# Batched matmul on one core: from a scheduled kernel to one critical section with hand-made waits, a TensorE loop, one load per stationary tile and the first x in one transfer

## The chip, the core and the metric

The kernel runs on one NeuronCore of a Trainium2 chip. Five engines work side by side, each with its own instruction stream: TensorE (PE; its weight loads have a row of their own, PEld), VectorE (DVE), ScalarE (ACT), GpSimd (POOL) and SyncE (SP). Here POOL and SP issue the transfers, which 16 DMA engines carry out. The metric is device time in microseconds of the whole launch; lower is better. Three runs of the kernel before took 513.78, 513.84 and 513.95 us, a median of 513.84 us.

## The reference

```python
batch, m, k, n = 32, 512, 1024, 768
x      = randn(batch, m, k)   float32
weight = randn(batch, k, n)   float32
out = np.matmul(x, weight)    # float32, (32, 512, 768)
```

The 32 matrices of weight are all different, so nothing is used twice across batches: 167.77 MB are read and 50.33 MB are written.

## The kernel before, in words

**Layout.** P is 128, MT = 4 tiles of rows, KT = 8 tiles of the contraction. A weight matrix is read as float32 and stored as bf16 by the transfer itself (1.5 MB in SBUF, 3.1 MB in memory). x is read in the same way; batches 1 and 2, 3 and 4, up to 29 and 30 are read in pairs, with batch 2p+1 in the lower and 2p+2 in the upper 64 partitions (L57, `load_pair`), and batch 31 alone (L62). Batch 0's x stays float32: three of its four row tiles come in one transfer from SP (L169), the fourth in 18 small ones of 16, 2 or 5 rows (L170 to L172).

**TensorE.** x must be turned before it can be the stationary operand. `words` (L74) transposes two bf16 at a time as if they were one float32: four transposes into one PSUM tile, eight such groups for a pair of batches. DVE copies each group into xT (L96; L93 and L94 for the last pair, L101 for batch 31, L115 for batch 0). `matmuls` (L128) then does, for each of 4 row tiles and 8 contraction tiles, two matmuls on the same stationary tile, 512 and 256 columns wide; each has its own weight load. So a batch has 64 matmuls and 64 loads. For batch 28 (`CHUNKED`, L29) the weight comes as two transfers, and the first half of the contraction is done for all row tiles before the second.

**Emptying PSUM.** Two row tiles share three PSUM banks. `evacuate` (L151) copies them to out_sb: ACT takes banks 0 and 2, DVE bank 1, each in two halves of 64 partitions (L163), whole for the batches 30 and 31 (L154 to L156).

**Order.** The order within each engine is written out by hand (`manual_schedule`, L165); the waits are put in by the framework from the pools: 4 weight buffers, 3 x buffers, 3 out buffers of a pair of batches, 6 of xT. POOL's queue holds, at an odd batch b: x of the pair that begins at b+4 (L190), the store of the pair that ended at b-2 (L192), the weight of b+3 (L194); at an even b only the weight of b+3. The weight of b+3 goes into the buffer of b-1, so it waits for the matmuls of b-1. The x of a pair takes the buffer of three pairs before, whose transposes are long done. From batch 26 on no store is issued until b = 28, when two are (L196, L197). The last stores are on SP: half of batch 30, the pair 28 and 29, the other half of 30, and two halves of 31 (L200 to L202, L232).

Of the kernel before, what the change touches and what calls it, by code (L numbers as in the profile page):

```python
# [13 lines left out]
def kernel(  # L14
# [9 lines left out]
    P = 128  # L24
    MT = M // P
# [3 lines left out]
    CHUNKED = {B - 4: (4, 4)}  # L29
    AHEAD = 3  # L30
    LATE = 4
    HELD = 3

    const = ctx.enter_context(tc.tile_pool(name="const", bufs=1))
    w_pool = ctx.enter_context(tc.tile_pool(name="w", bufs=4))
    x_pool = ctx.enter_context(tc.tile_pool(name="x", bufs=3))
    xT_pool = ctx.enter_context(tc.tile_pool(name="xT", bufs=6))
    out_pool = ctx.enter_context(tc.tile_pool(name="out", bufs=3))
    one_pool = ctx.enter_context(tc.tile_pool(name="one", bufs=1))
    tpsum = ctx.enter_context(tc.tile_pool(name="tpsum", bufs=2, space=bass.MemoryType.PSUM))  # L40
    mpsum = ctx.enter_context(tc.tile_pool(name="mpsum", bufs=2, space=bass.MemoryType.PSUM))

# [7 lines left out]
    xs, ws, outs, twos = {}, {}, {}, {}  # L52

    def banks():
        return [mpsum.tile([P, 512], F32, name=f"pm{i}") for i in range(3)]

    def load_pair(b):  # L57

        xs[b] = x_pool.tile([P, 2 * MT, K], BF16, name="x_sb")
        nc.gpsimd.dma_start(out=xs[b], in_=pair_view[b // 2])  # L60

    def load_last():  # L62
        xs[B - 1] = x_pool.tile([P, MT, K], BF16, name="x_sb")
        nc.gpsimd.dma_start(out=xs[B - 1], in_=x_view[B - 1])

    def load_w(b):
        ws[b] = w_pool.tile([P, KT, N], BF16, name="w_sb")
        at = 0
        for n in CHUNKED.get(b, (KT,)):
            nc.gpsimd.dma_start(out=ws[b][:, at:at + n, :], in_=w_view[b, :, at:at + n, :])  # L70
            at += n


    def words(b, mo):  # L74
        pt = tpsum.tile([P, JT, P], F32, name="pt")
        pairs = xs[b].bitcast(F32)
        for j in range(JT):
            nc.tensor.transpose(pt[:, j, :], pairs[:, mo, j::JT], ident)  # L78
        return pt.bitcast(BF16)

    def transpose_pair(b, mt):

        both = xT_pool.tile([P, 2, JT, 2, P // 2, 2], BF16, name="xT")
        in_rows = [both[:, r].rearrange("p j h i r -> p j (h i) r") for r in range(2)]
        if b + 1 == B - 2:

            in_rows[1] = both[:, 1].rearrange("p j h i r -> p j (h i r)").rearrange(
                "p j (m r) -> p j m r", r=2
            )
        for half in range(2):  # L90
            pt = words(b, mt + MT * half).rearrange("p j (b i r) -> p j b i r", b=2, r=2)
            if b + 1 == B - 2:
                nc.vector.tensor_copy(both[:, 0, :, half], pt[:, :, 0])  # L93
                nc.vector.tensor_copy(in_rows[1][:, :, half::2, :], pt[:, :, 1])  # L94
            else:
                nc.vector.tensor_copy(both[:, :, :, half].rearrange("p b j i r -> p j b i r"), pt)  # L96
        return in_rows

    def transpose_last(mt):
        xT = xT_pool.tile([P, JT, P, 2], BF16, name="xT")  # L100
        nc.vector.tensor_copy(  # L101
            xT.rearrange("p j m r -> p (j m r)"), words(B - 1, mt).rearrange("p j m -> p (j m)")
        )
        return xT

    def transpose_first(mt):

        xT = xT_pool.tile([P, JT, P, 2], BF16, name="xT")
        rows = x_first[:, mt] if mt < MT - 1 else x_fourth[:, 0]
        for h in range(2):  # L110
            pt = tpsum.tile([P, JT, P], F32, name="pt")
            for i in range(JT):
                nc.tensor.transpose(pt[:, i, :], rows[:, JT * h + i::KT], ident)  # L113
            for j in range(2):
                nc.vector.tensor_copy(  # L115
                    xT[:, 2 * h + j].rearrange("p (h i) r -> p r h i", h=2),
                    pt[:, 2 * j:2 * j + 2].rearrange("p r (i h) -> p r h i", h=2),
                )
        return xT


# [6 lines left out]
    def matmuls(pm, half, xT, b, kos, together):  # L128
        for ko in kos:
            for i, (bank, at, off, size) in enumerate(SPLITS[half]):  # L130
                shares = half == 1 and i == 0
                nc.tensor.matmul(  # L132
                    pm[bank][:, at:at + size],
                    xT[:, ko // 2, :, ko % 2],
                    ws[b][:, ko, off:off + size],
                    start=(ko == 0 and not (together and shares)),
                    stop=(ko == KT - 1),
                    skip_group_check=together,
                )

    def open_out(b):

        if b == B - 2:
            outs[b] = one_pool.tile([P, MT * N], F32, name="one_sb")
            return
        if b % 2 == 0 or b == B - 1:
            twos[b // 2] = out_pool.tile([P, 2 * MT * N], F32, name="out_sb")
        if b == B - 1:
            outs[b] = twos[b // 2][:, :MT * N]

    def evacuate(b, pair, pm):  # L151
        if b >= B - 2:
            o = outs[b][:, pair * N2:(pair + 1) * N2]
            nc.scalar.copy(o[:, 0:512], pm[0])  # L154
            nc.vector.tensor_copy(o[:, 512:1024], pm[1])  # L155
            nc.scalar.copy(o[:, 1024:N2], pm[2])  # L156
            return
        H = P // 2
        mine = twos[b // 2][H * (b % 2):H * (b % 2 + 1)]
        for i, copy in enumerate((nc.scalar.copy, nc.vector.tensor_copy, nc.scalar.copy)):  # L160
            for h in range(2):
                at = pair * N2 + h * MT * N + 512 * i
                copy(mine[:, at:at + 512], pm[i][H * h:H * (h + 1)])  # L163

    with tc.manual_schedule():  # L165

        x_first = x_pool.tile([P, MT - 1, K], F32, name="x_sb")
        x_fourth = one_pool.tile([P, 1, K], F32, name="one_sb")
        nc.sync.dma_start(x_first, x_view[0, :, :MT - 1])  # L169
        few = [slice(at, first + 20, 4) for first in (0, 20, 40) for at in range(first, first + 4)]  # L170
        for rows in (slice(64, 80), slice(80, 96), slice(96, 112), slice(112, P), slice(60, 62), slice(62, 64), *few):
            nc.sync.dma_start(x_fourth[rows, 0], x_view[0, rows, MT - 1])  # L172
        load_w(0)
        ident = const.tile([P, P], F32)
        make_identity(nc, ident)
        load_pair(1)
        load_w(1)
        load_w(2)
        load_pair(3)

        def store(at):
            nc.gpsimd.dma_start(out=two_view[at], in_=twos[at])  # L182

        ready = {}
        for b in range(B):
            if b % 2 and b + AHEAD + 1 < B:
                if b + AHEAD + 1 == B - 1:
                    load_last()
                else:
                    load_pair(b + AHEAD + 1)  # L190
            if b % 2 and 2 < b < B - HELD - AHEAD:
                store((b - 3) // 2)  # L192
            if b + AHEAD < B:
                load_w(b + AHEAD)  # L194
            if b == B - LATE:
                store(b // 2 - 2)  # L196
                store(b // 2 - 1)  # L197
            if b == B - 1:
                halves = [slice(pair * N2, (pair + 1) * N2) for pair in range(2)]
                nc.sync.dma_start(out_view[b - 1, :, halves[0]], outs[b - 1][:, halves[0]])  # L200
                nc.sync.dma_start(two_view[b // 2 - 1], twos[b // 2 - 1])
                nc.sync.dma_start(out_view[b - 1, :, halves[1]], outs[b - 1][:, halves[1]])  # L202
            open_out(b)
            if b == 0:
                xT = {mt: transpose_first(mt) for mt in range(MT - 1)}
            elif b == B - 1:
                xT = {mt: transpose_last(mt) for mt in range(MT)}
            else:
                if b % 2:
                    for mt in range(MT):  # L210
                        ready[b, mt], ready[b + 1, mt] = transpose_pair(b, mt)
                xT = {mt: ready.pop((b, mt)) for mt in range(MT)}
            if b in CHUNKED:
                pms = [banks() for _ in range(2)]
                at = 0
                for n in CHUNKED[b]:
                    for mt in range(MT):
                        matmuls(pms[mt // 2], mt % 2, xT[mt], b, range(at, at + n), True)
                        if at + n == KT and mt % 2 == 1:
                            evacuate(b, mt // 2, pms[mt // 2])  # L220
# [42 lines left out]
```

## Time and profile before

| what | value |
|---|---|
| median of the runs shown | 513.84 us |
| the profiled execution: its time, its span | 513.74 us, 511.9 us |
| mean granted TensorE clock | 0.953 |
| busy: PE, PEld, DVE, ACT, POOL | 425.1, 276.6, 171.8, 145.4, 34.3 us |
| transfers on POOL's queue, on SP's | 96.4%, 4.1% of 16 engines' span |
| last PE matmul, last ACT copy begins | 502.5 us, 503.05 us |

The span runs from the first to the last instruction on the chip; the execution's time has 1.8 us more around it. A group in the profile is named by line, engine and operation and by the names of its tiles: "pm<-w_sb,xT" is a matmul into PSUM tile pm from the weight and xT. The profile's view of waits says which engine waited for whom; the chain is the sequence of work that ended last, followed back from the end. The trace also records when each of the 16 DMA engines reported its part of a transfer as landed.

### The profile page before, as it was taken

How to read it: one execution, taken by the hardware profiler on the slowest of the kernel's cores; microseconds unless marked ns; L12 is line 12 of the kernel's file. 1: busy time of each engine (PE TensorE's matmuls, PEld its weight loads, DVE VectorE, ACT ScalarE, POOL GpSimd, SP SyncE). 2: the span in 40 equal slices, each digit the busy share in tenths (PEclk: the TensorE clock that was granted, in tenths of full speed). 3: DMA queues.
4: the chain of work that ended last, by engine and by line, in shares of the span. 5: the costliest groups of instructions: out<-in, count | busy, mean ns of one | idle time of the engine just before them, and what ended most of it. 6: DMA issues, size and time to landing. Idle time of an engine off the chain costs nothing.

```text
span 511.9 us, 5954 instructions
## 1 busy us (share of the span) xinstructions
PE 425.1 (83%) x2528; PEld 276.6 (54%) x2576; DVE 171.8 (34%) x272; ACT 145.4 (28%) x249; POOL 34.3 (7%) x69
## 2 busy tenths in 40 slices
PE   1804998989898989997888878887888879898992
PEld 1503666665656665653656446464465645666661
DVE  0302426253525252431525315252152621615230
ACT  1200242414242423332242322323223232232310
POOL 3000010101010101000010000101001000010000
PEclk9956999999999999997999989999799998999997
DMA  8999999999999999999999999999999999999997
GB/s 238 224 222 214 220 217 217 335 221 317 235 223 331 216 327 229 230 325 220 329 224 242 313 223 333 217 253 300 219 338 215 266 289 219 333 219 217 325 428 338
DMA packets 10218, 135.65 MB, mean 265 GB/s; under 512 B 1232, under 2 KB 1232, under 8 KB 2128
## 3 DMA queue, kind: packets, MB, share of 16 engines
q0 software_dynamic: 9072, 126.88, 96.4%
q1 hardware_dynamic: 1120, 8.39, 4.1%
q8 instruction: 20, 0.33, 0.2%
q14 instruction: 6, 0.05, 0.0%
HBM read 167.77 MB, written 50.33 MB: 426 GB/s over the span
## 4 chain that ended last, share of the span: by engine, by line
PE 45%; DMA 37%; issue 9%; DVE 5%; another core or an unknown queue 1%; POOL 0%; SPq 0%; ACT 0%; POOLq 0%
PE pm L132 40%; DMA w_sb<-in_weight_dram 29%; DMA one_sb<-in_x_dram 8%; PE pt L78 5%; DVE xT L96 3%; DVE out_sb L163 1%; PE pt L113 0%; DVE xT L93 0%; POOL out_dram L182 0%; DVE xT L94 0%; DVE one_sb L155 0%; DVE xT L101 0%; ACT out_sb L156 0%; SPq L172 0%
## 5 line engine op out<-in xcount | busy, mean ns | idle before, releaser
L132 PE MATMUL pm<-w_sb,xT 128*128 128x256 bf16 (+1 forms) x2000 | 343.8, 330 | 24.8 <-DMA w_sb<-in_weight_dram 22.3
L132 PEld LDWEIGHTS <-xT 128*128 128x128 bf16 x2048 | 203.3, 99 | 160.6 <-issue 33.0
L163 ACT COPY out_sb<-pm 64x512 f32<-64x512 f32 x240 | 139.5, 581 | 339.4 <-PE pm L132 286.1
L163 DVE COPY out_sb<-pm 64x512 f32<-64x512 f32 x120 | 82.6, 688 | 267.7 <-PE pm L132 185.9
L78 PE MATMUL pt<-ident,x_sb 128*128 128x128 f32 x496 | 79.9, 302 | 21.7 <-DVE xT L96 19.7
L78 PEld LDWEIGHTS pt<-ident,x_sb 128*128 128x128 f32 x496 | 69.3, 209 | 32.9 <-DVE xT L96 27.7
L96 DVE COPY xT<-pt 128x1024 bf16<-128x1024 bf16 x112 | 72.2, 687 | 10.6 <-PE pt L78 10.2
L70 POOL DMA_DIRECT2D w_sb<-in_weight_dram x33 | 17.7, 536 | 403.0 <-PE pm L132 402.2
L113 PE MATMUL pt<-ident,one_sb 128*128 128x128 f32 x8 | 1.9, 422 | 20.5 <-DMA one_sb<-in_x_dram 20.5
L115 DVE CAST xT<-pt 128x256 bf16<-128x256 f32 x16 | 6.0, 441 | 35.3 <-PE pt L113 35.1
L113 PE MATMUL pt<-ident,x_sb 128*128 128x128 f32 x24 | 4.9, 363 | 10.9 <-DMA x_sb<-in_x_dram 10.4
L113 PEld LDWEIGHTS pt<-ident,one_sb 128*128 128x128 f32 x8 | 1.6, 218 | 20.8 <-issue 20.8
L113 PEld LDWEIGHTS pt<-ident,x_sb 128*128 128x128 f32 x24 | 3.9, 206 | 11.7 <-issue 10.4
L60 POOL DMA_DIRECT2D x_sb<-in_x_dram x15 | 8.1, 540 | 11.0 <-PE pt L113 11.0
L182 POOL DMA_DIRECT2D out_dram<-out_sb x14 | 7.5, 538 | 5.7 <-issue 4.8
L155 DVE COPY out_sb<-pm 128x512 f32<-128x512 f32 x2 | 1.4, 692 | 8.8 <-PE pm L132 8.8
L155 DVE COPY one_sb<-pm 128x512 f32<-128x512 f32 x2 | 1.4, 692 | 8.3 <-PE pm L132 8.3
L93 DVE COPY xT<-pt 128x512 bf16<-128x512 bf16 x8 | 3.4, 421 | 0.7 <-PE pt L78 0.7
L94 DVE COPY xT<-pt 128x512 bf16<-128x512 bf16 x8 | 3.3, 415 | 0.0
L154 ACT COPY out_sb<-pm 128x512 f32<-128x512 f32 x2 | 1.2, 587 | 6.5 <-PE pm L132 6.5
L101 DVE COPY xT<-pt 128x1024 bf16<-128x1024 bf16 x4 | 2.6, 685 | 0.2 <-PE pt L78 0.2
L156 ACT COPY one_sb<-pm 128x512 f32<-128x512 f32 x2 | 1.2, 587 | 4.2 <-PE pm L132 4.2
(10 smaller groups left out, 5.1 us busy)
## 6 DMA issues: line engine op xcount, KB each, us to landing
w_sb<-in_weight_dram POOLq DMA_DIRECT2D x31, 1536.0 KB, 40.2
out_dram<-out_sb POOLq DMA_DIRECT2D x14, 3072.0 KB, 51.3
x_sb<-in_x_dram POOLq DMA_DIRECT2D x15, 2048.0 KB, 47.1
out_dram<-out_sb SPq DMA_DIRECT2D x1, 3072.0 KB
x_sb<-in_x_dram SPq DMA_DIRECT2D x1, 1536.0 KB
w_sb<-in_weight_dram POOLq DMA_DIRECT2D x2, 768.0 KB, 50.4
out_dram<-one_sb SPq DMA_DIRECT2D x2, 768.0 KB
out_dram<-out_sb SPq DMA_DIRECT2D x2, 768.0 KB
```

The lines of the kernel that those rows point to most:

```text
L60: nc.gpsimd.dma_start(out=xs[b], in_=pair_view[b // 2])
L70: nc.gpsimd.dma_start(out=ws[b][:, at:at + n, :], in_=w_view[b, :, at:at + n, :])
L78: nc.tensor.transpose(pt[:, j, :], pairs[:, mo, j::JT], ident)
L93: nc.vector.tensor_copy(both[:, 0, :, half], pt[:, :, 0])
L94: nc.vector.tensor_copy(in_rows[1][:, :, half::2, :], pt[:, :, 1])
L96: nc.vector.tensor_copy(both[:, :, :, half].rearrange("p b j i r -> p j b i r"), pt)
L113: nc.tensor.transpose(pt[:, i, :], rows[:, JT * h + i::KT], ident)
L115: nc.vector.tensor_copy(xT[:, 2 * h + j].rearrange("p (h i) r -> p r h i", h=2), pt[:, 2 * j:2 * j + 2].rearrange("p r (i h) -> p r h i", ...
L132: nc.tensor.matmul(pm[bank][:, at:at + size], xT[:, ko // 2, :, ko % 2], ws[b][:, ko, off:off + size], start=(ko == 0 and not (together an ...
L155: nc.vector.tensor_copy(o[:, 512:1024], pm[1])
L163: copy(mine[:, at:at + 512], pm[i][H * h:H * (h + 1)])
L182: nc.gpsimd.dma_start(out=two_view[at], in_=twos[at])
```

## The change

The tile pools and the scheduler are gone. All buffers and PSUM tiles are allocated by hand, and everything runs in one critical section in which each engine has its own list of instructions and semaphores of the program's own.

- x buffers are 2, not 3 (batch 0's x lies in an out buffer); xT buffers are those of one pair; weight and out buffers are as many as before.
- TensorE's instructions for batches 1 to 28 are a loop with 7 passes over four batches; batches 0, 29 to 31 stand outside it. The other engines' lists stay written out.
- The second matmul on a stationary tile is added as an instruction that has no weight load.
- SP waits for each load in turn and passes it on to TensorE through one semaphore for weights and one for x.
- Batch 0's x comes in one transfer; all of it is transposed before the first matmul. Batch 28's weight comes in one transfer, its matmuls in the usual order.
- The second half of PSUM bank 2 is copied by DVE, not by ACT, except in batches 30 and 31.
- At the end POOL resets the semaphores of its transfers.

```diff
-    CHUNKED = {B - 4: (4, 4)}
+    GROUPS = 2 * MT
+    W_SLOTS, X_SLOTS, OUT_SLOTS = 4, 2, 3
+    LOOPS = (B - 4) // W_SLOTS
+    LOOPED = 2 * LOOPS
...
+    x_first = outs[2][:, :MT * K].rearrange("p (mo k) -> p mo k", mo=MT)
...
     def load_w(b):
+        if b >= W_SLOTS:
+            pool.wait_ge(s_mm, mm_done(b - W_SLOTS))
+        pool.dma_start(out=ws[b % W_SLOTS], in_=w_view[b]).then_inc(s_w[b % W_SLOTS], 16)
+
+    def load_x(k):
+        if k >= X_SLOTS:
+            pool.wait_ge(s_pt, pt_done(k - X_SLOTS))
+        slot = xs[k % X_SLOTS]
...
+    def other(out, weights, moving, first, last):
+
+        return pe.add_instruction(
+            mybir.InstMatmult(
...
+                ldweights=False,
             )
...
+    def multiply(b, mt):
+        pm, half = pms[mt // 2], mt % 2
+        xT, w = stationary(b, mt), ws[b % W_SLOTS]
+        for ko in range(KT):
             for i, (bank, at, off, size) in enumerate(SPLITS[half]):
...
+                if i:
+                    last = other(*args, ko == 0, ko == KT - 1)
+                else:
+                    last = pe.matmul(*args, start=(ko == 0), stop=(ko == KT - 1))
+        last.then_inc(s_mm, 1)
...
+    def pair_on_pe(k, q):
+
+        b = 2 * k + 1
+        take(s_xr)
+        for g in range(GROUPS):
+            if GROUPS * q + g > 1:
+                pe.wait_ge(s_c, GROUPS * q + g - 1)
+            transpose(b, g)
+        for r in range(2):
+            take(s_wr)
+            for mt in range(MT):
+                at = 4 * q + 2 * r + mt // 2
+                if not r:
+                    pe.wait_ge(s_c, GROUPS * q + 2 * mt + 2)
+                pe.wait_ge(s_a, at + 1 + mt % 2)
...
+                multiply(b + r, mt)
...
+        with pe.Fori(0, LOOPS):
+            for q in range(2):
+                pair_on_pe(q, q)
+            pe.wait_ge(s_c, 2 * GROUPS).then_inc(s_c, -2 * GROUPS)
+            pe.wait_ge(s_a, 9).then_inc(s_a, -8)
+            pe.wait_ge(s_d, 9).then_inc(s_d, -8)
+        pair_on_pe(LOOPED, 0)
...
+    def out_on_dve(b, p):
+        j = 2 * b + p
+        if p == 0:
+            slot_free(dve, b)
+        dve.wait_ge(s_mm, 2 * j + 2)
...
+        for piece in pieces(b, p, 1):
+            last = dve.tensor_copy(*piece)
+        last.then_inc(s_d, 1)
+        dve.tensor_copy(*pieces(b, p, 2)[1]).then_inc(s_dp, 1)
...
+    def landed(what, i):
+
+        slots, ready = what
+        sp.wait_ge(slots[i % len(slots)], 16 * (i // len(slots) + 1))
+        sp.sem_inc(ready, 1)
...
         for b in range(B):
             if b % 2 and b + AHEAD + 1 < B:
-                if b + AHEAD + 1 == B - 1:
-                    load_last()
-                else:
-                    load_pair(b + AHEAD + 1)
+                load_x((b + AHEAD) // 2)
             if b % 2 and 2 < b < B - HELD - AHEAD:
-                store((b - 3) // 2)
+                a = (b - 3) // 2
+                store(pool, a, s_st[a % OUT_SLOTS])
             if b + AHEAD < B:
                 load_w(b + AHEAD)
...
+        used = range(sems[0].num, s_fin.num)
+        pool.dma_reset(used)
+        pool.sem_clear(used)
+
+    with tc.tile_critical():
+        sp.dma_start(x_first, x_view[0]).then_inc(s_first, 16)
+        on_pool()
+        on_pe()
+        on_dve()
+        on_act()
+        on_sp()
+        clear_on_pool()
```

## The prediction

> **What bounds the kernel now.** I first read the page's slices and queues.
>
> ```profile
> DMA  8999999999999999999999999999999999999997
> ...
> q0 software_dynamic: 9072, 126.88, 96.4%
> q1 hardware_dynamic: 1120, 8.39, 4.1%
> q8 instruction: 20, 0.33, 0.2%
> ```
>
> The 16 DMA engines are busy in every slice but the first and last. The landing records say the same in steady state: the weight of batch 24 landed at 391.31 us, of 25 at 398.58, then x at 408.31, a store at 415.59, the weight of 26 at 422.81. So a pair of batches costs 31.5 us of transfers (7.27 + 9.73 + 7.28 + 7.22). PE needs 27.2 us for it (matmuls began at 83.05 and at 110.25). Next, the waits:
>
> ```profile
> POOL w_sb L70 <- PE pm L132: 402.2, 28, 33.2
> ...
> PE pm L132 <- DMA w_sb<-in_weight_dram: 22.3, 7, 4.5
> ```
>
> POOL waits 402 us for buffers, but that starves nobody: a load lands a median of 40.2 us after its issue, so four or five transfers are always queued. PE waits seven times for a weight. The end, from the timeline and the windows:
>
> ```profile
> 422.95 12.24 PE L132 MATMUL pm<-w_sb,xT 128*128 128x512 bf16 x63 [4.14 <-DMA w_sb<-in_weight_dram]
> ...
> 441.43 20.96 PE L132 MATMUL pm<-w_sb,xT 128*128 128x512 bf16 x125
> ...
> 469.05 20.96 PE L132 MATMUL pm<-w_sb,xT 128*128 128x512 bf16 x125
> ...
> 492.45 10.56 PE L132 MATMUL pm<-w_sb,xT 128*128 128x512 bf16 x62
> ...
> 503.05 0.59 ACT L156 COPY out_sb<-pm 128x512 f32<-128x512 f32 x1 [2.12 <-PE pm L132]
> ```
>
> ```profile
> 500.00:504.00 4.00, 2.96 (x18) 1.59 (x17) 0.69 (x1) 1.17 (x2) 0.00 (x0) 1.00 0.96 412
> 504.00:508.00 4.00, 0.00 (x0) 0.00 (x0) 0.00 (x0) 0.00 (x0) 0.00 (x0) 0.64 0.99 413
> 508.00:512.00 4.00, 0.00 (x0) 0.00 (x0) 0.00 (x0) 0.00 (x0) 0.00 (x0) 0.50 0.38 158
> ```
>
> After its last wait (at 422.95, weight of 26) PE runs nearly without a gap to 503; the transfers stay saturated past it (0.99 in 504 to 508, the column before the GB/s). The 16 engines report the last store at 508.25 to 511.00 us. So **transfers bound the kernel from 1.75 us, the first packet, to 511.0**, and PE stands close behind: its last store, issued at 503.99, found a queue still busy.
>
> **The change, part by part.** Sums are against the profiled execution (513.74 us: span 511.9 and 1.8 around it), which is 0.1 below the median of the runs; I add that 0.1 at the end.
>
> *Bytes.* They stay the same, so the 31.5 us per pair stay. Batch 0's x is 128 rows of 4 KB more or less in one piece; its tail no longer holds PE until 44 us, but PE then only waits for weights instead: worth 0, as the DMA engines were busy meanwhile (0.93 up to 16 us, 1.02 up to 44). If that cover were gone it would be 20 us, PE's wait there.
>
> *Two x buffers.* This moves issues on POOL's queue. At odd b the x of b+4 now waits for the transposes of b, and the store and the weight of b+3 stand behind it. Before, x was issued when the matmuls of b-2 ended. Does the queue run dry? When the weight of b-1 lands, weight b, x, a store, and weights b+1 and b+2 are still queued: 3 x 7.27 + 9.73 + 7.28 = 38.8 us. The matmuls of b-1 (10.56) and the transposes (6.24 from matmul to matmul before, about 7 after) come first: x is issued 17.5 us later, with 21 us still queued. The first POOL transfer took 4.6 us from issue (1.26) to its first packet (5.84). So 21 covers it by 16 us: cost 0.
>
> *DVE.* Half of bank 2 moves to it: one copy of 64x512, 0.69 us (row L163 DVE, 688 ns), stands ahead of the transposes' copies once per pair. PE's pair becomes 27.9 us, its wait per pair 3.6. Cost 0 in steady state, 0.7 at the end.
>
> *One load per stationary tile.* 1024 loads of 99 ns go (row L132 PEld). They lie beside matmuls: a window of full work has PE busy 7.95 of 8.00 us, and 50 matmuls take 8.18 us in the chain, 327 ns a step of 768 columns. No row shows a matmul without its load. Bounds: 99 ns a step gained, or 99 lost, if the remaining load can no longer run ahead. I take 0, by the gapless row.
>
> *The loop.* The trace fetched 20 instruction blocks of 16 KB, 231 to 286 PE instructions apart: 256 each. A pass has 4 x 96 + 128 = 512 instructions plus branches and waits, just over two blocks. 4128 instructions are executed in place of 5152. If every pass is fetched anew, three blocks or so each, the fetches are 3 x 7 + 3 = 24, as many as before. One fetch keeps one DMA engine 0.94 us: 20 of them are 1.2 us a engine of 16, the main part of the spread of 2.75 us at the end. I take no change. A jump back may also stall PE until its block is there; no row shows one. Bounds: 0, and 15.0 us, the longest that the chain waits for small transfers beside POOL's (one_sb, at 14.22). I take 4.6, by the nearest row: SP's half store, issued at 485.47 under load, had its first packet at 489.15 (3.7), and a block takes 0.94. There are six jumps, each with two waits of 3.6 us to absorb it, so the cost is 0 up to 7.2 us a jump. The Trainium skill ("Runtime: NRT & Kernel Launch", Instruction fetch mechanics) says that a taken branch whose target is outside a window of two blocks must fetch it before going on, which speaks against this loop; by it the jump stalls, but the sum above holds at any stall under 7.2.
>
> *The end.* Without chunks batch 28 waits for its whole weight, 454.7 us, not the first half, 451.3; PE had begun it at 452. From there, with the rows above: relay over SP 0.2 (454.9); matmuls of 28, half of 20.96; to the next pair's matmuls 6.66 (462.39 to 469.05) + 0.69; 20.96; 2.43; 10.56; ACT 0.63. That is 507.3. Then 0.35 to the issue, 1.0 to the first packet (SP's first, 0.74 to 1.75), 8 packets of 234 ns per engine (1.87), 0.35 to the landing: **510.9, where the transfers end at 511.0 anyway.** The cover is exactly used up: whatever delays PE further after 454.7 counts in full.
>
> *Entry and exit.* The critical section adds a meeting of all engines at each end. The nearest rows are SP waiting for PE in the present ones, 0.7 us at the start and 0.7 at the end. Bounds 0 and 0.7 each; I take 0.2 and 0.3, since engines are there already. SP's 49 relays run on an engine that has nothing else to do; POOL's reset comes while the last store drains.
>
> Sum: 513.74 - 0.1 + 0.5 = 514.1, with 0.1 to the median **514.2 us**.
>
> **Rivals.**
> - *Cold clock at batch 28.* PE's wait there is some 3.6 us. Before, waits of 3.88 to 4.55 us were followed by a clock of 0.5 and matmuls of 12.24 to 13.21 us in place of 10.56; waits of 1.51 to 2.47 were not. The Trainium skill ("TensorE: Matmul & The Clock Gate", Part 1: The HAM clock gate) puts the window at about 3.4 us, free-running; by that it is near a coin's toss. Against it: a cold batch shortens the next wait, so that they alternated. Price 1.7 to 2.65 us: 515.9 to 516.9.
> - *The jump makes PE the bound* (slower). Place: the six jumps back. It decides from 7.2 us a jump; at 10 us it costs 6 x 2.8 = 17 us (531), at 8 us 5, at 15 us 47. An exposed load would do the same: 64 x 99 ns = 6.3 us a pair against 3.6. For it: nothing in the trace shows a jump. Against: the 4.6 us above, and the 21 us of queued transfers, which a late issue must use up first.
> - *Blocks stay with PE* (faster). If the loop is not fetched again, some 5 fetches remain, and the rows of batch 0's x, of which five engines had 12 to 14 more, are even. The earliest engine's landing, 508.25, plus 4 rows of 165 ns and one fetch is 509.9; the weight of 28 comes 1 to 1.8 us sooner, and PE's path ends at 509.1 to 509.9. So 1.1 to 1.9 less: 512.4 to 513.2. Against it: fetches every 256 instructions up to the end look like a small store.
> - *The second load is still made.* Then PE is as before and the blocks are more: 514.2 too.
>
> **How the numbers follow.** A measurement of this kernel can tell about 0.2% from no change: 512.81 to 514.87. My forecast has 0.40 (its own range 513.5 to 514.9, from the entry and exit bounds: faster 0.04, same 0.33, slower 0.03). Cold clock 0.22, slower. Jump or exposed load 0.13, slower. Blocks kept 0.20 (faster 0.13, same 0.07). Load still made 0.05 (same 0.04, faster 0.01). So faster 0.18, same 0.44, slower 0.38. The range runs from the faster rival to the upper end of the cold one, 512.3 to 517.0; outside are the jump and a little of the faster one, 0.16.
>
> **What would show it.** DMA at 9 in all slices and weights 31.5 us apart per pair: bytes and x buffers right; a dip after a jump: wrong. PE at 327 ns a step: load hidden. Fewer than 10 packets on q8: blocks kept. A clock of 0.5 after 454 us: cold. The last ACT copy beginning near 506.7: the end right. If weights land further apart than 31.5 us, the forecast falls, and the jump or the loads are to blame.

## The result, and the profile after

Twelve runs of the changed kernel took 514.16 to 517.45 us, a median of **515.01 us**; twelve of the kernel before, beside them, 513.78 to 513.95, a median of 513.87. The ratio is 1.0027 (95% interval 1.002 to 1.0035): slower by 1.14 us. The time lies in the predicted range, but 0.14 us past 514.87, where the prediction had drawn the line of "slower". What catches the eye is the spread: 0.17 us before, 3.3 us after. The profiled execution took 515.77 us, with a span of 513.8.

The slices and queues of the changed kernel's page:

```profile
DMA  8999999999999999999999999999999999999995
...
q0 software_dynamic: 8928, 126.88, 96.0%
q1 hardware_dynamic: 864, 8.39, 4.0%
q8 instruction: 4, 0.07, 0.0%
```

Until the last slice the transfers are as full as before; the last slice fell from 7 to 5. And q8 fetched 4 instruction blocks, not 20. The waits, in us in total, times, the longest:

```profile
POOL x L101 <- PE pt L171: 272.6, 13, 33.6
...
POOL w L92 <- PE pm L126: 124.9, 14, 9.6
...
PE pm L158 <- PEq L175: 29.9, 12, 3.8
```

POOL now waits mostly for the transposes, as two x buffers make it; PE waits twelve times for a weight (L175 is `take`, the wait for a relayed weight), never over 3.8 us. The weight of batch 24 landed at 391.48 us, of 26 at 423.00, of 28 at 454.61: 31.5 and 31.6 us a pair, as before (454.69). What differs comes after that. The timeline and the windows of the changed kernel at batch 28; in a window the columns are its length, then busy us of PE, PEld, DVE, ACT and POOL, the granted clock, the share of the DMA engines and GB/s:

```profile
454.94 0.38 PE L158 MATMUL pm<-w,xT 128*128 128x512 bf16 x1 [2.45 <-PEq L175]
```

```profile
450.00:455.00 5.00, 2.49 (x15) 0.68 (x7) 1.99 (x3) 1.65 (x3) 1.06 (x2) 1.00 1.00 211
455.00:459.00 4.00, 4.00 (x16) 0.93 (x9) 0.00 (x0) 0.00 (x0) 0.54 (x1) 0.60 0.99 210
459.00:463.00 4.00, 3.95 (x24) 1.20 (x12) 0.91 (x2) 1.74 (x3) 0.00 (x0) 0.97 1.03 215
```

PE is equally busy in the last two windows, but got through 16 recorded matmuls in one and 24 in the other: the clock was 0.5 from 455.8 to 459.2 us, and batch 28 took 12.24 us (454.94 to 467.18) where a warm batch takes 10.56. Then the end:

```profile
500.00:504.00 4.00, 4.00 (x27) 1.18 (x12) 0.50 (x1) 1.15 (x2) 0.00 (x0) 1.00 0.92 390
504.00:508.00 4.00, 3.95 (x26) 1.27 (x13) 0.19 (x1) 0.60 (x2) 0.00 (x0) 1.00 0.62 253
508.00:512.00 4.00, 0.60 (x4) 0.00 (x0) 0.69 (x1) 0.58 (x1) 0.00 (x0) 1.00 0.47 194
```

Before, PE was done at 503 and the transfers stood at 0.99 until 508. Now PE works until 508.6 and the transfers have run out beside it, 0.62: **the end has changed its owner**. The last pieces of the chain say the same; the last copy, by DVE, ends at 509.32, and the last store lands at 512.68:

```profile
508.38 0.23 PE pm L126
508.61 0.02 issue
508.63 0.69 DVE out L294
```

### The profile page after: what moved, and what is told of

The parts are those of the page before. It is cut to its first block, busy times and chain, and to the rows that moved or that the text cites. A ratio compares the mean times of both kernels' runs of the same rounds, so it can differ in the third digit from the quotient of the medians.

```text
span 513.8 us, 5039 instructions
## 1 busy us (share of the span) xinstructions
PE 428.7 (83%) x2528; PEld 178.5 (35%) x1552; DVE 209.8 (41%) x332; ACT 110.1 (21%) x189; POOL 33.7 (7%) x68
## 5 line engine op out<-in xcount | busy, mean ns | idle before, releaser
L158 PE MATMUL pm<-w,xT 128*128 128x512 bf16 (+1 forms) x993 | 301.6, 328 | 32.4 <-PEq L175 29.9
L126 PE MATMUL pm<-w,xT 128*128 128x256 bf16 (+1 forms) x1007 | 303.8, 327 | 2.1 <-issue 0.7
L158 PEld LDWEIGHTS pm<-w,xT 128*128 128x128 bf16 x1024 | 101.4, 99 | 265.5 <-issue 257.7
L297 DVE COPY out<-pm 64x512 f32<-64x512 f32 x120 | 82.6, 689 | 252.9 <-PE pm L126 252.1
L283 ACT COPY out<-pm 64x512 f32<-64x512 f32 (+1 forms) x122 | 70.7, 579 | 301.0 <-PE pm L126 300.3
L171 PE MATMUL pt<-ident,x 128*128 128x128 f32 x496 | 87.5, 326 | 32.3 <-DVE xT L251 29.2
L171 PEld LDWEIGHTS pt<-ident,x 128*128 128x128 f32 x496 | 73.4, 210 | 49.7 <-DVE xT L251 40.1
L286 ACT COPY out<-pm 64x512 f32<-64x512 f32 (+1 forms) x62 | 35.8, 578 | 89.1 <-PE pm L126 89.1
L299 DVE COPY out<-pm 64x512 f32<-64x512 f32 x60 | 41.2, 686 | 0.0
L101 POOL DMA_DIRECT2D x<-in_x_dram x15 | 8.0, 532 | 272.8 <-PE pt L171 272.6
L92 POOL DMA_DIRECT2D w<-in_weight_dram x32 | 17.2, 538 | 125.9 <-PE pm L126 124.9
L171 PE MATMUL pt<-ident,out 128*128 128x128 f32 x32 | 6.3, 348 | 13.1 <-DMA out<-in_x_dram 12.5
L109 POOL DMA_DIRECT2D out_dram<-out x14 | 7.5, 536 | 1.4 <-DVE out L299 1.3
## 6 DMA issues: line engine op xcount, KB each, us to landing
x<-in_x_dram POOLq DMA_DIRECT2D x15, 2048.0 KB, 29.3
```

The source lines that it names most:

```text
L92: pool.dma_start(out=ws[b % W_SLOTS], in_=w_view[b]).then_inc(s_w[b % W_SLOTS], 16)
L101: pool.dma_start(out=slot, in_=pair_view[k]).then_inc(s_x[k % X_SLOTS], 16)
L109: eng.dma_start(out=two_view[a], in_=outs[a % OUT_SLOTS]).then_inc(sem, 16)
L126: return pe.add_instruction(mybir.InstMatmult(name=nc.get_next_instruction_name(), engine=mybir.EngineType.PE, ins=[pe.lower_ap(moving), p ...
L158: last = pe.matmul(*args, start=(ko == 0), stop=(ko == KT - 1))
L171: last = pe.transpose(pts[g % 2][:, i, :], rows, ident)
```

## The theory and its rivals

Theory: batch 28's weight in one piece makes PE the last to end. The 16 DMA engines then no longer cover what PE loses to a cold clock, and this is the spread and most of the median. The loop's few instruction fetches gain about as much as the one big transfer of the first x loses. Rivals: the cost is in the matmul without a load, in DVE's extra copies, in the x buffers, or in a stall at the loop's jump. The last can be read from the trace without a run. Here is the jump at 149 us in the changed kernel's timeline, from the last matmul of one pass to the transposes that open the next:

```profile
149.27 0.38 PE L126 MATMUL pm<-w,xT 128*128 128x512 bf16 x1
149.49 0.51 PE L171 MATMUL pt<-ident,x 128*128 128x128 f32 x3
```

From start to start it takes 0.22 us, and so (0.21 or 0.22) do all 16 such steps, jump or no jump. There is no stall.

## Experiments on the end

**Batch 28's weight in two transfers again, in the changed kernel.** The last pass of the loop is written out for it.

```diff
+        if b == B - 4:
+            pool.dma_start(out=ws[0][:, :4, :], in_=w_view[b, :, :4, :]).then_inc(s_w[0], 16)
+            pool.dma_start(out=ws[0][:, 4:, :], in_=w_view[b, :, 4:, :]).then_inc(s_half, 16)
+            return
...
+            if b + r == B - 4:
+                take(s_wr)
+                for mt in range(MT):
+                    multiply(b + r, mt, range(4, KT), True)
...
-        with pe.Fori(0, LOOPS):
+        with pe.Fori(0, LOOPS - 1):
```

> The changed kernel with the weight of batch 28 in two transfers again and its matmuls in two halves of the contraction; the loop's last pass is written out for that. Theory (late, cold start of batch 28): PE begins batch 28 at about 452.5 instead of 454.9 us, after a wait under 1 us and at full clock, its last matmul ends near 504 instead of 508.6, and the transfers set the end again: 513.6 to 514.3 us with rounds within 0.5 us of each other. Rival (the critical section itself, its entry, exit and relays, cost the 1.1 us): batch 28 does not matter and the time stays at 515.0 with rounds from 514.2 to 517.

Measured: 513.75 us (513.4 to 514.25), ratio to before 0.9999 (0.999 to 1.0008). So 1.26 us less than the changed kernel by the medians, and the spread is down to 0.85. Its windows at the end:

```profile
504.00:508.00 4.00, 1.30 (x8) 0.24 (x3) 0.69 (x1) 0.58 (x1) 0.00 (x0) 1.00 0.87 364
508.00:512.00 4.00, 0.00 (x0) 0.00 (x0) 0.00 (x0) 0.00 (x0) 0.00 (x0) 0.80 0.26 104
```

PE's work ends at 505.3, the transfers go on to 510.77: the owner is the DMA again. This edit carries the whole loss, and not by an earlier weight: the second half of batch 28's landed at 454.84, the whole one in the changed kernel at 454.61, and the pass written out costs two more blocks (6 on q8). Everything else in the change sums to nothing that can be told (-0.1 us).

**The same in the kernel before: one transfer for batch 28.**

```diff
-    CHUNKED = {B - 4: (4, 4)}
+    CHUNKED = {}
```

> The kernel before with one transfer for batch 28's weight, nothing else. Theory: PE starts batch 28 some 2.6 us later and, in runs with a clock of 0.5 there, 1.7 us more; but before's last store had 3.8 us of cover (ACT done at 503.64, 3.6 us to the landing, 511.0), so most of it is swallowed: 513.9 in warm runs, up to 514.5 in cold ones. Rival (the missing chunks alone are the whole 1.1 us): 515.0.

Measured: 514.68 us (513.79 to 515.84), ratio 1.0017 (1.0008 to 1.0025). The sign holds and the spread grows from 0.9 (before, beside it) to 2.1 us, but the median is past the expected upper end: the kernel before has less cover than was worked out. The profiled execution was one of the lowest (513.79; its batch 28 ran warm, 10.56 us after a wait of 2.64), so its trace doesn't show where the upper runs lose. The mean clocks of the twelve runs point to the cold clock: the five runs at 0.951 or 0.952 took 514.98 to 515.84 us, the seven at 0.957 to 0.960 took 513.79 to 514.77.

**Keeping the clock up.** Eight more matmuls whose result nobody reads, ahead of the wait for each even batch's weight: first in the loop and before batch 30, then in the loop alone (`range(8 * r * (k < LOOPED))`).

```diff
         for r in range(2):
+            for _ in range(8 * r):
+                pe.matmul(
+                    pts[0].rearrange("p j m -> p (j m)"),
+                    stationary(b, 0)[:, 0, :, 0],
+                    both[1].rearrange("p a j h i r -> p (a j h i r)")[:, :512],
+                    start=True,
+                    stop=True,
+                )
             take(s_wr)
```

> The changed kernel with 8 more matmuls of 128x512 (their result is never read) ahead of the wait for the weight of each even batch in the loop and of batch 30, some 1.7 us of work where PE waits 1.6 to 3.3 us. Theory: no clock of 0.5 at batch 28, its matmuls take 10.56 us, PE's path ends 1.7 us sooner than in the profiled run: 514.1 to 514.8 with rounds within 0.6 us (batch 30, which has no wait to hide them, loses 1.7 us if PE is the bound there, so up to 515.3 at most). Rival (the clock is not the cause of the spread between 514.2 and 517.4): spread and median as now.

> As the run with 8 more matmuls ahead of each even batch's weight, but only up to batch 28, not ahead of batch 30, where nothing hid them: 8 x 216 ns = 1.7 us off PE's path. Theory: no clock of 0.5 at batch 28 and PE's path of 52.4 us from its weight: 514.2 to 514.7 us, all rounds within 0.5 us. Rival: as wide as the changed kernel, 514.2 to 517.

Measured: the first 516.15 us (515.94 to 516.47), ratio 1.0043 (1.003 to 1.0056); the second 514.36 (513.77 to 514.92), ratio 1.0007 (0.9999 to 1.0016). In the second one's timeline and windows at batch 28:

```profile
451.33 1.89 PE L187 MATMUL pt<-xT 128*128 128x512 bf16 x8
454.82 0.38 PE L158 MATMUL pm<-w,xT 128*128 128x512 bf16 x1 [1.60 <-PEq L175]
```

```profile
455.00:459.00 4.00, 4.00 (x26) 1.27 (x13) 0.00 (x0) 1.16 (x2) 0.00 (x0) 1.00 0.97 206
```

The clock stays at 1.00 and 26 matmuls are done where there were 16. The spread shrinks from 3.3 to 1.15 us (0.5 was expected) and the median by 0.65. But the clock does not stay up to the end: in this execution it fell to 0.5 at 470.35, again for 3.4 us, as the window shows.

```profile
470.00:474.00 4.00, 4.00 (x19) 2.83 (x18) 3.07 (x9) 0.00 (x0) 0.00 (x0) 0.57 1.08 227
```

There it fell mostly on transposes of the next pair: 24 of them took 5.37 us in place of 4.61. From batch 28's first matmul to PE's last it is 52.87 us here and 53.66 in the changed kernel: 0.8 less, not the whole 1.68. So the 0.65 is what it is worth to move the cold stretch to a cheaper place; a kernel without one was not run.

The first version's upper bound of 515.3 was missed, and that is telling too. Batch 30 waits for no weight, so there the eight stand on PE's path:

```profile
483.75 1.89 PE L187 MATMUL pt<-xT 128*128 128x512 bf16 x8
485.47 0.38 PE L158 MATMUL pm<-w,xT 128*128 128x512 bf16 x1
```

Batch 30's first matmul comes 1.72 us later for them, and the time is 1.8 us longer (516.15 against 514.36): after batch 28 every delay of PE counts in full.

**ACT copies the second half of bank 2 again.** VectorE makes a copy of 128x8 for its semaphore.

```diff
-        act.copy(*pieces(b, p, 2)[0]).then_inc(s_ap, 1)
+        for piece in pieces(b, p, 2):
+            last = act.copy(*piece)
+        last.then_inc(s_ap, 1)
...
-        dve.tensor_copy(*pieces(b, p, 2)[1]).then_inc(s_dp, 1)
+        dve.tensor_copy(spare[:, 8 * j:8 * j + 8], ident[:, :8]).then_inc(s_dp, 1)
```

> The changed kernel with the second half of PSUM bank 2 copied by ACT again (DVE makes a copy of 128x8 in SBUF in its place, for its semaphore). Theory: PE's pair is 0.6 us shorter, so PE's path to the end is 0.6 us shorter, but each wait for a weight is 0.6 us longer, so a clock of 0.5 at batch 28 is no rarer: 513.9 when warm, 515.2 when cold, median 514.3 to 515.2. Rival (DVE's extra copies are the cost): 514.2 or less in every round.

Measured: 514.83 us (513.38 to 516.53), ratio 1.0017 (1.0007 to 1.0027). The median is 0.2 below the changed kernel's with the same wide spread. That can't be told from nothing; the bulk of the loss is not there.

**Both: two transfers for batch 28, and ACT's copies.** This was the candidate to beat both kernels.

> The changed kernel with the weight of batch 28 in two transfers (as in e1_chunk) and, beside it, ScalarE copying the second half of every bank 2 again, as in the kernel before; VectorE only makes a small SBUF copy of 128x8 in its place. Theory: with two transfers the landing of the last store is set by the transfers, and in the profile of e1_chunk the last copy of ScalarE ended at 505.3 us, 5.4 us ahead of the last landing, so who copies bank 2 moves nothing: 513.4 to 514.0 us, no difference from the 513.75 of e1_chunk that can be told. Rival: the copy of VectorE at the very end (0.69 us in the profile) is part of what the last store waits for, and its removal shows whole: 513.0 to 513.3 us. If it comes out over 514.3 us, the extra copies of ScalarE (32 of some 0.7 us) hold up the banks of TensorE, which the waits of the profile would show.

(The 505.3 us in this text is when the last copies of that kernel begin.) Measured: 514.13 us (513.63 to 514.7), 0.1 past the expected range, beside a before of 514.13 on that chip; ratio 0.9999 (0.999 to 1.0009), the same as without the edit. The last piece of its chain:

```profile
504.48 0.69 DVE out L322
```

PE's path is 0.85 us shorter than with DVE's copies (505.33), and the last landing is at 510.99 as against 510.77. Where the transfers own the end, a shorter path of PE buys nothing. No version here beats the kernel before by anything that can be measured.

## Experiments on the loop and the loads

**The loop written out.**

```diff
-        with pe.Fori(0, LOOPS):
+        for turn in range(LOOPS):
             for q in range(2):
-                pair_on_pe(q, q)
+                pair_on_pe(2 * turn + q, q)
```

> The changed kernel with TensorE's loop written out, the same instructions in the same order. Theory (late, cold start of batch 28): the instruction blocks are fetched as they were before, 14 to 16 times instead of 4, but the weight of batch 28 still lands near 454.6 us and PE's path still sets the end: 514.2 to 517, median 514.7 to 515.3. Rival (the loop's jumps cost time): the median falls to 514.3 or less. Rival (the kept blocks are a gain that hides a larger loss elsewhere): it rises to 516 or more.

Measured: 516.39 us (515.33 to 517.38), ratio 1.0046 (1.0033 to 1.0058): 1.4 us more than with the loop by the medians, so the second rival (the kept blocks are a gain that hides a loss) was right. The size is uncertain: both kernels spread by 2 to 3 us, and the intervals of their ratios touch. The version with three x buffers below, also written out, took 517.02. The page of this one has

```profile
q8 instruction: 17, 0.28, 0.2%
```

and its weight of batch 28 landed at 455.46, 0.85 us later than with the loop. Batch 28 was cold in both profiles, so the landing explains 0.85 of the 0.92 us between these two executions; the rest of the 1.4 between the medians is not explained.

**A load of its own for every matmul.**

```diff
-                    last = other(*args, ko == 0, ko == KT - 1)
+                    last = pe.matmul(*args, start=(ko == 0), stop=(ko == KT - 1))
```

> The changed kernel with a weight load for every matmul again, the loop kept. Theory: a step of 768 columns stays at 327 ns, nothing moves on PE's path: median 514.7 to 515.3 us. Rival (the single load is worth some ns a step): the 112 steps from batch 28 on count in full, so 10 ns each would give 516.1. The body of the loop is then about 640 instructions of PE; if it is still not fetched again, PE holds at least that much.

Measured: 515.28 us (514.11 to 515.83), ratio 1.0026 (1.0014 to 1.0037), the same as the changed kernel. Its groups of weight loads, and its fetches:

```profile
q8 instruction: 5, 0.08, 0.1%
...
L158 PEld LDWEIGHTS pm<-w,xT 128*128 128x128 bf16 x1024 | 101.6, 99 | 101.4 <-issue 37.8
...
L156 PEld LDWEIGHTS pm<-w,xT 128*128 128x128 bf16 x1024 | 101.3, 99 | 64.5 <-issue 0.5
```

The 1024 loads are back (L156), 101 us of them, and cost nothing that can be told: they lie beside matmuls. A pass is now 640 instructions and is still fetched once.

**Three x buffers, in the kernel with the loop written out.**

```diff
-    W_SLOTS, X_SLOTS, OUT_SLOTS = 4, 2, 3
+    W_SLOTS, X_SLOTS, OUT_SLOTS = 4, 3, 3
```

> The written-out version of the changed kernel (516.39 us) with three x buffers instead of two. Theory: two buffers cost nothing, because a late x still finds some 20 us of queued transfers ahead of it: 515.3 to 517.4 with a median within 0.6 us of 516.39. Rival (the late issue of x is part of the loss): the median falls by 1 us or more.

Measured: 517.02 us (515.83 to 517.24), ratio 1.0049 (1.0035 to 1.0063), against 516.39 with two: no gain, so two buffers cost nothing that can be told.

## Experiments on the first x

**One transfer for it, in the kernel before.**

```diff
-        x_first = x_pool.tile([P, MT - 1, K], F32, name="x_sb")
-        x_fourth = one_pool.tile([P, 1, K], F32, name="one_sb")
...
+        x_first = x_pool.tile([P, MT, K], F32, name="x_sb")
+        nc.sync.dma_start(x_first, x_view[0])
```

> The kernel before with batch 0's x in one transfer, nothing else. Theory: PE starts its second batch some 20 us sooner and waits for weights instead, so the transfers' end decides. The five DMA engines with 12 to 14 more rows are relieved by up to 1.6 us and the eleven others get 0.65 us more; with the same 20 instruction blocks on all of them the slowest engine ends 0 to 0.5 us sooner: 513.3 to 513.9 us. Rival (an earlier PE meets more waits and more clock drops, one of them late): 514.3 or more.

Measured: 514.83 us (514.58 to 515.24), ratio 1.0018 (1.0009 to 1.0027): slower by 0.96. The expected gain is not there. The rival's number came true but not its reason: in the profile no cold stretch lies between 440 us and the end of PE's work, and the last copy began at 503.49 (503.05 before). The landing records say why. The 16 engines reported the last store at 507.72 to 511.93 us, before at 508.25 to 511.00: the last engine is 0.93 later, while PE was done long before. This table has, for the weight of batch 28 (its second half where it comes in two), when the 16 DMA engines reported it:

| kernel | first x | blocks on q8 | mean of 16 | last of 16 |
|---|---|---|---|---|
| before | 1 + 18 small | 20 | 453.75 | 454.69 |
| before, one x | 1 | 20 | 453.53 | 455.80 |
| after, loop written out | 1 | 17 | 453.50 | 455.46 |
| after | 1 | 4 | 452.51 | 454.61 |

A wait ends with the *last* engine. In the kernel before, five engines carry 12 to 14 rows of x more than the others. Without the 18 small transfers the mean is 0.2 earlier and the last engine 1.1 later; that the extra rows went to engines that would else run ahead is argued from this, not shown. Fewer fetches then bring the mean forward by 1.0 and the last by 0.85.

In the changed kernel the way to these 2.77 us between the first and the last engine can be followed in the landings: 0.7 us at 25.6 us, with only the first x behind; 1.9 at 34.1, one engine, just after the first instruction block at 31.7; a second engine 1.5 back at 68.0, after the block at 61.3; then 2.4 at 202 and 2.8 at 454, again two engines apart from the other 14. What sets an engine back is not made good later in this kernel.

**The same evening-out in the changed kernel**: 112 rows in one transfer, then 5, 5, 5 and 1; and this with batch 28 in two transfers.

```diff
-        sp.dma_start(x_first, x_view[0]).then_inc(s_first, 16)
+        for rows in (slice(0, 112), slice(112, 117), slice(117, 122), slice(122, 127), slice(127, 128)):
+            sp.dma_start(x_first[rows], x_view[0, rows]).then_inc(s_first, 16)
```

> The changed kernel with batch 0's x in five transfers: 112 rows over all 16 DMA engines (7 rows of 16 KB each), then three transfers of 5 rows and one of 1 row, which go to the first engines. So 11 engines get 7 rows instead of 8 (0.61 us less) and five get 10 or 11 (1.2 to 1.8 us more). Theory: what counts is the slowest of the 16 engines, which is 2.6 us behind the first because it fetched instruction blocks early, and the first five engines are not among those: the weight of batch 28 lands 0.4 to 0.6 us sooner (454.0 to 454.2 us) and PE's path ends as much sooner: median 514.3 to 514.7. Rival (the mean load of the engines counts): no change, 515.0; or the slow engines are among the first five: 516.2.

> The same uneven first x with the two transfers for batch 28's weight: both repairs. Theory: the transfers set the end, and their slowest engine is 0.4 to 0.6 us sooner: 513.1 to 513.4 us, less than the kernel before (513.87) by 0.1%. Rival (the first five engines are the slow ones): 515.

Measured: 518.5 us (517.62 to 519.1), ratio 1.0082 (1.0068 to 1.0096), and 517.56 (516.74 to 517.71), ratio 1.0066 (1.0052 to 1.008). Both expectations were wrong, and by far. PE's wait for the first x in the changed kernel, and in the first of these two:

```profile
PE pt L171 <- DMA out<-in_x_dram: 12.5, 1, 12.5
```

```profile
PE pt L171 <- DMA out<-in_x_dram: 24.2, 1, 24.2
```

The x came twice as late. The landing records say where. The 112 rows were reported at 11.37 to 12.50 us, hardly later than all 128 in one transfer (10.96 to 12.33). But the three transfers of 5 rows came one after another, at 15.5 to 16.3, 17.8 to 18.9 and 20.8 to 22.0, and the single row at 24.07. In the first 26 us the 16 KB packets took a mean of 934 ns each (722 in one transfer) and POOL's 12 KB packets beside them 1041 (926). The engines lay 5 us apart from then on, and the weight of batch 28 landed at 459.06, 4.5 us late; the time grew by 3.5. That is an unplanned test of the chain from the last engine to the end, which it bears out, but not of the evening-out, which stays untried in the changed kernel.

## Why the prediction was right in its range, and what it had wrong within it

The forecast was 514.2 us and "same" its likeliest class (0.44). The measured 515.01 lies 0.8 above the forecast, inside the range, and 0.14 past the line of "slower". Point by point, by its own steps:

- **Bytes**: 31.5 us a pair, right. That the one piece of x was worth 0 is wrong: in the kernel before it costs 0.96 us, through the last of the 16 engines. The step looked at who waits for x (nobody for long), not at which engines carry it.
- **Two x buffers**: 0, right. The x is issued a median of 29.3 us ahead of its landing (47.1 before), so that the queue never ran dry; three buffers gained nothing.
- **DVE**: 0.7 had been put into the sum, and the profiles show 0.5. Batch 28 is cold in the profiles of the changed kernel and of the one with ACT's copies; from its first matmul to PE's last it is 53.66 and 53.13 us. The medians (0.2 apart) can't tell this from 0. The place is PE's wait for the transposes' copies, before:

```profile
PE pt L78 <- DVE xT L96: 19.7, 42, 1.0
```

and after:

```profile
PE pt L171 <- DVE xT L251: 29.2, 31, 1.9
```

- **One load per stationary tile**: 0, right; still 327 ns a step.
- **The loop**: this step failed. It counted three blocks to fetch in each pass, 24 in all. The trace has 4, at 31.7, 61.3, 468.5 and 493.1 us: the code of a pass was fetched once and stayed. That is worth 1.4 us by the medians and 0.85 by the landing, and the rival that said so got the packets right and the sign wrong, since it took the even rows of the first x for a help where they cost. The 4.6 us that were allowed for a jump turned out to be none. The Trainium skill's rule ("Runtime: NRT & Kernel Launch", Instruction fetch mechanics) of a window of two blocks did not hold for this engine here, with passes of 512 and of 640 instructions and 0.22 us at each jump; the 128 KiB that the same section gives TensorE's instruction memory would hold such a pass.
- **The end**: the working held. Batch 28 began at 454.94 (454.9 predicted), the landing came 3.4 us after the last copy (3.6). The last copies began 1.9 us later than the 506.7 foretold: 1.68 of this is batch 28's cold clock (12.24 for 10.56), the rest small steps. Take the 1.68 off and this execution would be 514.1 us, an estimate that no run shows; the prediction said 514.2. (Its sum let the end come at 510.9, though by its own words the transfers end at 511.0: 0.1 too little.)
- **Entry and exit**: SP's first transfer was issued at 0.96 us (0.74 before), 0.2 as predicted; the span ends 1.13 us after the last landing (0.92), 0.2 where 0.3 was taken. The sum left the time outside the span at 1.8; over the twelve runs it was 2.07 on average (1.78 before), 0.3 that no term had.
- **Cold clock at batch 28**: priced rightly (1.7 to 2.65; measured 1.68), though PE's wait there was 2.45 us, not some 3.6. But it was given 0.22 as a case of its own, as if the kernel were either warm or cold. The same program is both, from one launch to the next, so the median carries a part of it: 0.65 us by the eight matmuls that move it away from batch 28.

The sum by the medians: whole weight and cold clock +1.26; entry and exit +0.4, first x +1.0 and loop -1.4, together 0. That is 1.3, or 1.6 with the 0.3 outside the span, against the 1.1 measured. The terms come from different kernels with a few tenths of doubt each, and the first x was measured only in the kernel before. So that the number came out within 0.8 us is in part luck: two missed terms had opposite signs.

Of the 1.26 us, 0.65 went when the cold stretch was moved away from batch 28. The other 0.6 is what a cold stretch at the transposes still costs and what PE's path costs even warm; no run here parts the two. For the second the profile gives some 0.2 (511.0, the last landing less the 1.68, against 510.77 with two transfers). Open is what moves the two late engines from 1.5 and 1.9 us behind, at 68 us, to 2.5 and 2.8 at 454, and what the first x in one piece costs in the changed kernel itself, where the one attempt to undo it slowed the transfers.

## What to carry to other kernels

Where saturated transfers own the end and another engine stands a few us behind, a "free" edit that delays this engine hands it the end, and with it all of its variance: look at the spread of the runs, not at the median alone. Count a transfer's cost on the slowest DMA engine, as a wait ends with the last of sixteen; moving the mean is not enough. A loop's price is in its trace: count the packets of the instruction queue and the step at the jump before arguing about either.

## What the runs showed of the hardware that was not expected

- **A wait of 2.45 us can cool the clock, and even one of 1.86.** In the changed kernel the first was followed by 0.5 from 455.8 to 459.2; other waits of up to 3.3 us in this kernel were not, nor was one of 2.64 in the kernel before with one transfer. Seven of the ten cold stretches up to the end of PE's work began within 2.2 us after a wait of 1.86 us between the transposes of a pair. In the kernel before, these waits are 1.0 to 1.2 us, and no cold stretch began there. The Trainium skill ("TensorE: Matmul & The Clock Gate", Part 1: The HAM clock gate) has a free-running window of about 3.4 us and asks for an idle one. The ten cold stretches are indeed 3.4 long, but PE's waits were shorter than that: the same length ahead of the one at 455.8 held 1.0 us of work, ahead of the ten 0.7 to 1.9 us.
- **Instruction blocks of a TensorE loop stay.** A loop of 7 passes over 512 or 640 instructions was fetched once: 4 and 5 packets on q8, against 17 with the passes written out.
- **A DMA engine's delay is kept.** In the changed kernel, with the transfers saturated, the last engine, set back just after an instruction block, is as far behind the first, or farther, hundreds of us later: 1.9 us at 34, 1.8 at 58, 2.4 at 202, 2.8 at 454.
- **Small SP transfers behind a large one came one after another.** After the 112 rows at 12.5 us the last reports of the transfers of 5, 5, 5 and 1 rows followed at 16.3, 18.9, 22.0 and 24.1: 2 to 4 us each for 16 rows in all, where 128 rows in one transfer had landed at 12.3.
